# Score and value matmuls of a head pair entered as one piece in the list scheduler

## The chip, the cores and the metric

The kernel runs on one core of one Trainium2 chip. The metric is the time on the device for one execution, in microseconds (us). A program computes the kernel's own instruction order when the kernel is built, so the order is the same in every run.

## The reference

One layer of a hybrid decoder, for 512 tokens of width 1024, all in float32. The inputs are normalised and multiplied by one wide input matrix. The columns of the product go to two branches: an mLSTM with 4 heads of 128, and an attention with 8 heads of 64. The two branch outputs are gated, laid side by side, and multiplied by an output matrix into the residual. The change touches the attention alone. With two blocks of 256 tokens and up to three past blocks chosen, every earlier block is chosen, so it is causal attention with a linear bias:

```python
q = _rmsnorm(at_q.reshape(B, S, 8, 64), q_norm_w)
k = _rmsnorm(at_k.reshape(B, S, 8, 64), k_norm_w)
s = einsum('bhqd,bhsd->bhqs', q, k) * 64 ** -0.5 - slopes * distance   # causal
o_at = einsum('bhqs,bhsd->bhqd', softmax(s), v)
y_at = o_at.reshape(B, S, 512) * silu(at_z)
```

## The kernel before

**Arithmetic.** A float32 matrix product is made of three passes of a faster format: each operand is split in a high part and a low part (`whi`, `wlo` for weights; `xh`, `xl` for activations), and `mm3` issues high by high, high by low, low by high. ScalarE writes the high part, VectorE the low part.

**Attention.** `g_pair(p)` handles heads 2p and 2p+1, for p = 0 to 3. TensorE transposes q and k of both heads at once, so that head 2p lies on partitions 0 to 63 and head 2p+1 on partitions 64 to 127; ScalarE and VectorE split them into `qh`, `ql`, `kh`, `kl` (tiles named `br`). `g_attn` then makes:

- Scores. For each of four blocks of 128 queries (`g_tile(i)`), six matmuls: three passes for each of the two heads, alternating between the heads in program order. One contracts 64 rows, so it occupies half of TensorE's rows, and each head has a PSUM bank of its own. The width is 256, 256, 384 and 512 columns for i = 0 to 3. That is 16 such sets in the kernel, 96 matmuls, shown as `bank<-br,br 64*128`.
- Softmax (`g_soft`): VectorE adds the bias and takes the minimum, ScalarE exponentiates, GpSimd multiplies by the reciprocal sum; then TensorE transposes the result (`bank<-ident,b`) and ScalarE and VectorE copy it back.
- Values. For each of four blocks j of 128 keys, one matmul per head with 64 output columns, so it occupies half of TensorE's columns; the two heads write the two halves of the partitions of one bank, `acc`. The width is 512, 384, 256 and 128 columns. One float32 call gives two records in the trace: 64 records in the kernel, shown as `bank<-b,vbuf 128*64`.

**Order.** While `nc.on` is set, every engine call goes through `Schedule.add`, which runs nothing: it notes the engine, an estimated cost, and for each tile region which earlier operations must be done before it. `Schedule.issue` then places all operations by list scheduling: `place` gives each engine, whenever it is free in the plan, the ready operation that is most urgent, and the pass is repeated backward and forward 12 times; the placement of the shortest span is kept. All operations are then issued in the order of their planned starts. Each engine executes its own queue in that order and waits on semaphores where an input isn't there. The plan's cost of a matmul on half the rows is half that of a whole one, and on half the columns likewise (0.21 in place of 0.43), whatever stands beside it in the order.

**What lies around the change.** While the attention runs, TensorE's queue also holds the projections of the mLSTM's q and k and of the gate (`bank<-xh,whi` and the like, with activations moving and weights fixed; 128x512). `whi,xh` and the like are the projections with weights moving. After the attention come the mLSTM's own products and the output projection.

Every operation that the scheduler issues carries the line of the call in `Schedule.add`, L257, in the profile; so groups are told apart by their tiles.

Of the kernel before, what the change touches and what calls it, by code (L numbers as in the profile page):

```python
# [189 lines left out]
class Schedule:  # L190
# [10 lines left out]

    def __init__(self, nc):
        self.nc, self.on, self.ops, self.log = nc, False, [], {}
        for name in ("vector", "scalar", "gpsimd", "tensor", "sync"):
            setattr(self, name, Taker(self, name, getattr(nc, name)))

# [44 lines left out]
    def add(self, eng, name, fn, args, kw):  # L251
        aps = [a for a in (*args, *kw.values()) if isinstance(a, bass.AP)]
        out = kw.get("out", args[0] if args else None)
        outs = [r for r in (self.region(a) for a in (out, kw.get("accum_out")) if a is not None) if r]
        ins = [r for r in (self.region(a) for a in aps if a is not out and a is not kw.get("accum_out")) if r]
        dma = name.startswith("dma")
        op = {"eng": eng, "fn": lambda: fn(*args, **kw), "cost": self.cost(eng, name, out, ins, args, kw), "n": len(self.ops),  # L257
              "table": next((self.TABLES[a] for a in args if isinstance(a, AF) and a in self.TABLES), 0) if name == "activation" else 0,
              "pre": {}}
        self.ops.append(op)  # L260
        done = op
        if dma:
            size = 4.0
            for d in out.shape:
                size *= d
            done = {"eng": "dma", "fn": None, "cost": size / 524288.0 * (2900.0 if kw.get("accum_op") else 1480.0), "n": len(self.ops),
                    "table": 0, "pre": {op["n"]: 0.0}}
            self.ops.append(done)
        for reg, write in [(r, False) for r in ins] + [(r, True) for r in outs]:
            log = self.log.setdefault(reg[0], [])  # L270
            for r, w, o in log:
                if (w or write) and r[1] < reg[2] and reg[1] < r[2] and r[3] < reg[4] and reg[3] < r[4]:
                    if o["n"] in (op["n"], done["n"]):
                        continue
                    lat = self.LAT[o["eng"]] if o["eng"] != eng else 0.0 if eng == "tensor" else self.OWN if w else 0.0
                    op["pre"][o["n"]] = max(op["pre"].get(o["n"], 0.0), lat)
            if write:
                log[:] = [e for e in log if e[2] in (op, done) or not (reg[1] <= e[0][1] and e[0][2] <= reg[2] and reg[3] <= e[0][3] and e[0][4] <= reg[4])]
            log.append((reg, write, done))
# [57 lines left out]
    def issue(self, rounds=12):  # L337
        self.on = False
        self.tables()
        for o in self.ops:  # L340
            o["cost"] *= self.RESERVE.get(o["eng"], 1.0)
        n = len(self.ops)
        edges = [list(o["pre"].items()) for o in self.ops]
        back = [[] for _ in range(n)]
        for i, pre in enumerate(edges):
            for j, lat in pre:
                back[j].append((i, lat))
        zero = [0.0] * n
        span = lambda s: max(t + o["cost"] for t, o in zip(s, self.ops))
        best = start = self.place(edges, list(range(n)), zero)  # L350
        for _ in range(rounds):
            late = self.place(back, [-(t + o["cost"]) for t, o in zip(start, self.ops)], zero)
            start = self.place(edges, [-(t + o["cost"]) for t, o in zip(late, self.ops)], zero)
            if span(start) < span(best):
                best = start
        for i in sorted(range(n), key=lambda i: (best[i], i)):
            if self.ops[i]["fn"]:
                self.ops[i]["fn"]()


class Taker:
# [15 lines left out]
def hybrid_layer(ctx: ExitStack, tc: tile.TileContext, xT, x, w_in, w_out, smalls, out):  # L377
    nc = Schedule(tc.nc)
# [66 lines left out]
    for name, cols in _chunks():  # L445
        n = len(cols)
# [389 lines left out]
    def g_attn(p, qh, ql, kh, kl, t0):  # L836
        rank = 5 + p / 100
        yield when(lambda: b2.ok() and b5.ok(2) and (p < 2 or 2 * p - 3 in pts))
        eh, prs = b2.get(), [b5.get() for _ in range(2)]

        te = pool.tensor_scalar(eh, dist, 2.0 ** -(2 * p + 1), 0.0, op0=ALU.mult, op1=ALU.add)
        mn, sums, rec = ([tiny(NT) for _ in range(2)] for _ in range(3))
        done = {"p": [0, 0], "t": [0, 0]}
        at = [t0, t0]

        def finish(key, u, t):
            at[u] = max(at[u], t)
            done[key][u] += 1

        def g_tile(i):  # L850
            n = P * (i + 1)
            nn = max(n, 256)
            yield (max(*at, te), lambda: banks.ok(KEEP + 1), True)
            ps = [banks.get() for _ in range(2)]
            ts = slice(i * P, (i + 1) * P)
            now = plan.now
            for a, b in ((qh, kh), (qh, kl), (ql, kh)):
                for u in range(2):
                    r = slice(64 * u, 64 * u + 64)
                    mm(ps[u][:, :nn], a[r, ts], b[r, :nn], a is qh and b is kh, a is ql)  # L860
            plan.now = (now + plan.now) / 2
            for u in range(2):
                plan.add(g_soft(u, i, n, ps[u]), rank, plan.now + SLACK)

        def g_soft(u, i, n, ps):
            p_ = prs[u][:, offs[i]:offs[i] + n]
            t_ = dve.tensor_tensor_reduce(p_, ps[:, :n], eh[:, S - n:], scale=-0.5 if u else -1.0, scalar=BIG,
                                          op0=ALU.add, op1=ALU.min, accum_out=mn[u][:, i:i + 1])
            banks.put(t_, ps)
            yield t_  # L870
            yield act.activation(p_, p_, AF.Exp, scale=-1.0, bias=mn[u][:, i:i + 1], accum_out=sums[u][:, i:i + 1])
            have["exp"] += 1
            dve.reciprocal(rec[u][:, i:i + 1], sums[u][:, i:i + 1])
            yield dve.clock + SLACK
            finish("p", u, pool.tensor_scalar(p_, p_, rec[u][:, i:i + 1], 1.0, op0=ALU.mult, op1=ALU.mult))

        def g_pt(u, a, blocks, pt):
            yield pe_bank(at[u])
            ps = banks.get()
            n = P * len(blocks)  # L880
            for b, (i, j) in enumerate(blocks):
                transpose(ps[:, b * P:(b + 1) * P], prs[u][:, offs[i] + j * P:offs[i] + (j + 1) * P], ident)
            yield plan.now + SLACK
            t_ = (act.copy, dve.tensor_copy, act.copy)[a](pt[:, 512 * a:512 * a + n], ps[:, :n])
            banks.put(t_, ps)
            finish("t", u, t_)

        def g_turn(u):
            yield when(lambda: done["p"][u] == NT and b5.ok())
            pt = b5.get()  # L890
            for a, blocks in enumerate(([(0, 0), (1, 0), (2, 0), (3, 0)],
                                        [(1, 1), (2, 1), (3, 1), (3, 3)],
                                        [(2, 2), (3, 2)])):
                plan.add(g_pt(u, a, blocks, pt), rank)
            yield when(lambda: done["t"][u] == 3)
            b5.put(plan.now, prs[u])
            pts[2 * p + u] = (pt, [pt[:, 0:512], pt[:, 512:896], pt[:, 1024:1280], pt[:, 896:1024]], at[u])

        for i in range(NT):
            plan.add(g_tile(i), rank)  # L900
        for u in range(2):
            plan.add(g_turn(u), rank + u / 200)
        yield when(lambda: sum(done["p"]) == 2 * NT)
        b2.put(plan.now, eh)
        br.put(plan.now, qh, ql, kh, kl)
        h = 2 * p + 1
        yield when(lambda: h in pts and h - 1 in pts and have["v"] == NT)
        yield pe_bank(max(pts[h][2], pts[h - 1][2]))
        acc = banks.get()
        for j in range(NT):  # L910
            for g in (h - 1, h):
                r0 = 64 * (g % 2)
                mm(acc[r0:r0 + 64, j * P:], tv[:, j, g * 64:g * 64 + 64], pts[g][1][j], j == 0, j == NT - 1)
            plan.now -= 4 * (S - j * P) / 2.4
            if j < NT - 1:
                yield pe()
        b5.put(plan.now, pts[h - 1][0], pts[h][0])
        yield plan.now + SLACK
        banks.put(dve.tensor_copy(ot[:, h // 2], acc), acc)
        have["at"] += 1  # L920
# [554 lines left out]
    for n, name in enumerate(NAMES):  # L1475
        if name not in SUMS:
            continue
        tag, other, op = SUMS[name]
# [136 lines left out]
```

## Time and profile before

| | |
|---|---|
| median of 3 runs | 311.43 us |
| lowest | 311.09 us |
| the profiled execution: time | 310.9 us |
| the profiled execution: span from the first to the last instruction | 309.2 us |
| TensorE busy | 304.3 us (98%) |
| VectorE busy | 215.5 us (70%) |
| ScalarE busy | 169.7 us (55%) |
| GpSimd busy | 68.8 us (22%) |

The busy times are sums over the span. PE is TensorE's matmuls, PEld its weight loads, DVE VectorE, ACT ScalarE, POOL GpSimd. A matmul's duration in the trace runs from its start until its last column is through, and the next one starts before that; so the distance from one start to the next start, and not the duration, is what a matmul takes of TensorE's time. "x6" in a row of the timeline is six records of one group with nothing of another group between them.

### The profile page before, as it was taken

How to read it: one execution, taken by the hardware profiler on the slowest of the kernel's cores; microseconds unless marked ns; L12 is line 12 of the kernel's file. 1: busy time of each engine (PE TensorE's matmuls, PEld its weight loads, DVE VectorE, ACT ScalarE, POOL GpSimd, SP SyncE). 2: the span in 40 equal slices, each digit the busy share in tenths (PEclk: the TensorE clock that was granted, in tenths of full speed). 3: DMA queues.
4: the chain of work that ended last, by engine and by line, in shares of the span. 5: the costliest groups of instructions: out<-in, count | busy, mean ns of one | idle time of the engine just before them, and what ended most of it. 6: DMA issues, size and time to landing. Idle time of an engine off the chain costs nothing.

```text
span 309.2 us, 4351 instructions
## 1 busy us (share of the span) xinstructions
PE 304.3 (98%) x1566; PEld 238.2 (77%) x1566; DVE 215.5 (70%) x457; ACT 169.7 (55%) x309; POOL 68.8 (22%) x90
## 2 busy tenths in 40 slices
PE   8999999999999999999999999999999999999995
PEld 4999888888886676766668657898888988788884
DVE  4987997789784576795656876183117767989992
ACT  3675847972456644364544469569132334679600
POOL 4000202159500465002525021100101037222200
PEclk9999999999999999999999999999999999999999
DMA  6995887334061010130001321446327389965434
GB/s 203 394 414 193 180 259 146 61 136 136 0 207 67 1 65 11 62 138 2 0 3 68 118 86 32 105 134 209 86 50 191 119 281 227 260 128 89 62 120 159
DMA packets 13381, 40.19 MB, mean 130 GB/s; under 512 B 1584, under 2 KB 1840, under 8 KB 13360
## 3 DMA queue, kind: packets, MB, share of 16 engines
q1 hardware_dynamic: 10640, 32.05, 29.7%
q0 software_dynamic: 2720, 7.87, 14.6%
q8 instruction: 12, 0.20, 0.3%
q14 instruction: 9, 0.07, 0.1%
HBM read 37.81 MB, written 2.10 MB: 129 GB/s over the span
## 4 chain that ended last, share of the span: by engine, by line
PE 98%; DVE 0%; issue 0%
PE bank L257 97%; PE bank L370 1%; DVE b L257 0%; DVE rstdb L370 0%; DVE warm L370 0%
## 5 line engine op out<-in xcount | busy, mean ns | idle before, releaser
L257 PE MATMUL bank<-whi,xh 128*128 128x512 f32 (+2 forms) x220 | 71.1, 364 | 0.0
L257 PE MATMUL bank<-wlo,xh 128*128 128x512 f32 (+2 forms) x220 | 71.0, 358 | 0.0
L257 PE MATMUL bank<-whi,xl 128*128 128x512 f32 (+2 forms) x220 | 71.0, 360 | 0.0
L257 DVE TENSOR_TENSOR wlo<-raw,whi 128x1024 fp32r<-128x1024 f32 x35 | 42.5, 1220 | 21.8 <-ACT whi L257 21.7
L257 PEld LDWEIGHTS bank<-whi,xh 128*128 128x128 f32 x220 | 38.5, 191 | 7.6 <-issue 0.8
L257 ACT CAST whi<-raw 128x1024 fp32r<-128x1024 f32 x35 | 36.4, 1048 | 12.5 <-PE bank L257 12.5
L257 PEld LDWEIGHTS bank<-whi,xl 128*128 128x128 f32 x220 | 38.2, 188 | 6.6 <-issue 0.2
L257 PEld LDWEIGHTS bank<-wlo,xh 128*128 128x128 f32 x220 | 38.2, 188 | 6.2
L257 PE MATMUL bank<-xh,whi 128*128 128x512 f32 x96 | 41.1, 428 | 0.0
L257 PE MATMUL bank<-xh,wlo 128*128 128x512 f32 x96 | 39.4, 411 | 0.0
L257 PE MATMUL bank<-xl,whi 128*128 128x512 f32 x96 | 39.3, 409 | 0.0
L257 PE MATMUL bank<-whi,br 128*128 128x512 f32 x112 | 36.3, 397 | 0.0
L257 POOL TENSOR_SCALAR b<-b,tinies 128x128 f32<-128x128 f32 (+3 forms) x32 | 23.1, 732 | 44.1 <-DVE tinies L257 40.3
L257 DVE CUSTOM_DVE_ANT_0 b<-bank,b 128x128 f32<-128x128 f32 (+3 forms) x32 | 15.0, 485 | 17.8 <-PE bank L257 17.8
L257 ACT ACTIVATE b<-b,tinies 128x128 f32<-128x128 f32 (+3 forms) x32 | 17.8, 556 | 16.0 <-DVE tinies L257 16.0
L257 PEld LDWEIGHTS bank<-whi,br 128*128 128x128 f32 x112 | 21.0, 188 | 5.0
L257 PEld LDWEIGHTS bank<-xh,whi 128*128 128x128 f32 x96 | 18.1, 188 | 6.1 <-issue 2.4
L257 PEld LDWEIGHTS bank<-xh,wlo 128*128 128x128 f32 x96 | 18.0, 188 | 5.8 <-issue 2.3
L257 PE MATMUL bank<-wlo,br 128*128 128x512 f32 x56 | 22.3, 399 | 0.0
L257 PEld LDWEIGHTS bank<-xl,whi 128*128 128x128 f32 x96 | 18.1, 189 | 4.3 <-issue 1.8
L257 POOL TENSOR_TENSOR tinies<-tinies,mhalf 128x8 f32<-128x8 f32 (+1 forms) x12 | 18.3, 1546 | 7.0 <-DVE tinies L257 6.8
L257 PE MATMUL bank<-ident,b 128*128 128x128 f32 (+1 forms) x104 | 18.5, 267 | 0.0
(170 smaller groups left out, 467.2 us busy)
## 6 DMA issues: line engine op xcount, KB each, us to landing
raw<-in_w_in_dram SPq DMA_DIRECT2D x28, 512.0 KB, 3.3
raw<-in_w_out_dram SPq DMA_DIRECT2D x5, 512.0 KB, 4.1
vbuf<-in_x_dram SPq DMA_DIRECT2D x4, 512.0 KB, 8.3
out_dram<-b SPq DMA_DIRECT2D x7, 256.0 KB, 2.1
b<-in_w_in_dram SPq DMA_DIRECT2D x3, 520.0 KB, 7.2
raw<-in_w_out_dram POOLq DMA_DIRECT2D x3, 512.0 KB, 6.5
b<-in_x_dram POOLq DMA_DIRECT2D x6, 256.0 KB, 4.3
tq<-in_xT_dram SPq DMA_DIRECT2D x4, 256.0 KB, 5.3
```

Source lines behind the costliest of these rows:

```text
L257: op = {"eng": eng, "fn": lambda: fn(*args, **kw), "cost": self.cost(eng, name, out, ins, args, kw), "n": len(self.ops), "table": next((se ...
L370: return fn(*args, **kw)
```

## The change

`Schedule` gets a `bundle`. While it is `None`, nothing differs. When it is a list, the first operation added becomes the piece that is scheduled, and each later one adds its cost to it and its call to the piece's list of calls. What the later ones must wait for, and what waits for them, is noted on the piece. `issue` runs the calls of a piece one after another, so nothing else stands between them in TensorE's queue. Two places use it: the six score matmuls of one block of queries, and the two value matmuls of one block of keys. The set of instructions, their operands and the plan's total cost are as before.

```diff
         self.nc, self.on, self.ops, self.log = nc, False, [], {}
+        self.bundle = None
...
-        op = {"eng": eng, "fn": lambda: fn(*args, **kw), "cost": self.cost(eng, name, out, ins, args, kw), "n": len(self.ops),
+        call = lambda: fn(*args, **kw)
+        op = {"eng": eng, "fn": [call], "cost": self.cost(eng, name, out, ins, args, kw), "n": len(self.ops),
...
-        self.ops.append(op)
+        if self.bundle is not None:
+
+            if not self.bundle:
+                self.bundle.append(op)
+            elif op is not self.bundle[0]:
+                self.bundle[0]["cost"] += op["cost"]
+                self.bundle[0]["fn"].append(call)
+            op = self.bundle[0]
+        if op["n"] == len(self.ops):
+            self.ops.append(op)
...
-            if self.ops[i]["fn"]:
-                self.ops[i]["fn"]()
+            for fn in self.ops[i]["fn"] or ():
+                fn()
...
             now = plan.now
+            nc.bundle = []
             for a, b in ((qh, kh), (qh, kl), (ql, kh)):
                 for u in range(2):
                     r = slice(64 * u, 64 * u + 64)
                     mm(ps[u][:, :nn], a[r, ts], b[r, :nn], a is qh and b is kh, a is ql)
+            nc.bundle = None
...
         for j in range(NT):
+            nc.bundle = []
             for g in (h - 1, h):
                 r0 = 64 * (g % 2)
                 mm(acc[r0:r0 + 64, j * P:], tv[:, j, g * 64:g * 64 + 64], pts[g][1][j], j == 0, j == NT - 1)
+            nc.bundle = None
```

## Rows read from the trace of the kernel before

**Rows 1.** The page: span, busy times, granted clock in 40 slices, chain that ended last.
```profile
span 309.2 us, 4351 instructions
...
PE 304.3 (98%) x1566; PEld 238.2 (77%) x1566; DVE 215.5 (70%) x457; ACT 169.7 (55%) x309; POOL 68.8 (22%) x90
...
PEclk9999999999999999999999999999999999999999
...
PE bank L257 97%; PE bank L370 1%; DVE b L257 0%; DVE rstdb L370 0%; DVE warm L370 0%
```

**Rows 2.** Waits of PE (all there are): us in total, times, longest.
```profile
PE bank L370 <- DVE warm L370: 1.2, 1, 1.2
```

**Rows 3.** Timeline of PE, 150.2 to 151.6: start, us, operation.
```profile
150.16 0.40 PE L257 MATMUL bank<-xl,whi 128*128 128x512 f32 x1
150.40 0.39 PE L257 MATMUL bank<-xh,wlo 128*128 128x512 f32 x1
150.72 0.61 PE L257 MATMUL bank<-br,br 64*128 64x256 f32 x3
151.26 0.51 PE L257 MATMUL bank<-xh,whi 128*128 128x512 f32 x1
151.60 0.40 PE L257 MATMUL bank<-xl,whi 128*128 128x512 f32 x1
```

**Rows 4.** Timeline of PE, 103.2 to 109.9.
```profile
103.27 0.62 PE L257 MATMUL bank<-br,br 64*128 64x256 f32 x6
103.82 0.50 PE L257 MATMUL bank<-xh,whi 128*128 128x512 f32 x1
...
106.84 0.79 PE L257 MATMUL bank<-br,br 64*128 64x384 f32 x3
...
109.83 0.97 PE L257 MATMUL bank<-br,br 64*128 64x512 f32 x6
```

**Rows 5.** Timeline of PE, first and last stretch of scores, and one in between.
```profile
95.23 0.74 PE L257 MATMUL bank<-br,br 64*128 64x256 f32 x6
...
100.34 0.96 PE L257 MATMUL bank<-br,br 64*128 64x512 f32 x3
...
159.71 0.97 PE L257 MATMUL bank<-br,br 64*128 64x512 f32 x6
```

**Rows 6.** Busy time by stretch (window, its length, PE busy, records), tile br alone: scores.
```profile
95.00:102.00 7.00, 4.17 (x24) 1.00 0.00 1
102.00:111.00 9.00, 3.77 (x24) 1.00 0.00 0
...
150.00:161.00 11.00, 5.01 (x24) 1.00 0.01 2
```

**Rows 7.** The same, tile vbuf alone: values.
```profile
120.00:125.00 5.00, 3.45 (x16) 1.00 0.28 99
132.00:139.00 7.00, 3.44 (x16) 1.00 0.37 133
170.00:174.00 4.00, 2.60 (x16) 1.00 0.00 0
```

**Rows 8.** Timeline of PE, stretches of values of the second and the last pair.
```profile
132.79 1.07 PE L257 MATMUL bank<-b,vbuf 128*64 128x512 f32 x2
...
136.47 2.37 PE L257 MATMUL bank<-b,vbuf 128*64 128x512 f32 x14
...
183.31 1.72 PE L257 MATMUL bank<-b,vbuf 128*64 128x512 f32 x8
...
185.86 0.87 PE L257 MATMUL bank<-b,vbuf 128*64 128x256 f32 x8
```

**Rows 9.** Waits of all engines: us in total, times, longest.
```profile
DVE b L257 <- PE bank L257: 34.7, 27, 5.1
```

**Rows 10.** Timeline of DVE, the third pair's low parts.
```profile
136.86 1.41 DVE L257 SCALAR_TENSOR_TENSOR br<-bank,sm,br 128x512 fp32r<-128x512 f32 x2
```

**Rows 11.** Timeline of PE, the scores that follow them.
```profile
138.76 0.62 PE L257 MATMUL bank<-br,br 64*128 64x256 f32 x6
```

## The prediction

> **What bounds the kernel now.** I read the page first. TensorE is busy for 304.3 of 309.2 us, the chain that ended last lies 97% on TensorE's matmuls of line 257, and the granted clock is at its upper level, 2.4 GHz, in every slice [rows 1]. Next I asked for TensorE's waits. There is one, of 1.2 us, at the warm-up ahead of the first weights [rows 2]. From there until its last matmul TensorE never stands still for an input. So the time of the kernel is that wait, plus what the matmuls take one after another, plus a tail behind the last one (a VectorE step and the last store). Whatever shortens TensorE's own sequence shortens the kernel by as much, until something else fails to keep up.
>
> So the question is what the half-array matmuls take today. For that I read TensorE's timeline by starts. A whole matmul of 512 columns is followed by the next after 0.24 us (150.16, 150.40) [rows 3]. At 150.72 stand three score matmuls of 256 columns together, and the next matmul starts 0.54 us later [rows 3]. At 103.27 six of the same width stand together and take 0.55 us, until 103.82 [rows 4]. So six cost what three cost: in the six, each head's matmul has the other head's beside it, while the three run one after another with half of the rows unused. The last record of such a stretch reaches 0.07 us over the next start (0.62 of busy time against 0.55) [rows 4]. Taken off, three of 384 columns (0.79) take 0.72 us and six of 512 (0.97) take 0.90 [rows 4]; three of 512 take 0.96 - 0.07 = 0.89, the same as six [rows 5].
>
> There is a second cost, of a stretch as such. The step from a whole matmul into a stretch is 0.32 us (150.40 to 150.72), and the first whole matmul behind it takes 0.34 (151.26 to 151.60) [rows 3]. Against 0.24 each that is 0.08 + 0.10, and to the nearest tenth 0.2 us for each stretch of half-array matmuls, beside its own length.
>
> **The change, part by part.** *Scores.* The 96 matmuls stand in 22 stretches today; the first begins at 95.23, the last at 159.71 [rows 5]. The four pairs of heads are busy for 4.17, 3.77, 3.77 (the second row of 3.77, from 138 to 149, isn't shown) and 5.01 us [rows 6], together 16.72; less 22 x 0.07 it is 15.18 us from start to start. After the change there are 16 whole sets, for each pair two of 256 columns, one of 384 and one of 512. I have no whole set of 384. Three alone take 0.72, six of the other widths cost what three do, and the middle between 0.55 and 0.90 is 0.72 as well, so I take 0.72. If halves of 384 did not overlap at all, a set would be 1.43, and the sum would lose 4 x 0.71 = 2.8 us; at the widths on both sides they do overlap, so that end gets almost no weight. One pair: 0.55 + 0.55 + 0.72 + 0.90 = 2.72; four pairs 10.88. Gain: 15.18 - 10.88 = 4.3 us.
>
> *Score stretches.* From 22 to 16, at 0.20 each: 1.2 us. Where two sets happen to be neighbours it is a little more.
>
> *Values.* The first two pairs are busy for 3.45 and 3.44 us, the last two for 2.60 and 2.59 (only the first of these is shown) [rows 7]. The difference is what a missing partner costs. In the last pairs the records stand eight and eight, both heads together; in the second pair two of one head go alone at 132.79, and 14 in an uneven order follow at 136.47 [rows 8]. All together it is 12.08 us of busy time in 9 stretches; less 9 x 0.07, 11.45. A pair as the last two takes 2.60 - 2 x 0.07 = 2.46, four of them 9.84. Gain: 1.6 us. The stretches go from 9 to 8, another 0.2, if key blocks stay two by two. They needn't: a piece here is one key block. If all 16 stand alone, there are seven stretches more than today, 1.4 us lost in place of 0.2 won; if the four of each pair stand together, there are four, and 1.0 is won. I take 8, the pattern of the two undisturbed pairs, and keep both ends (1.6 us worse, 0.8 better).
>
> *The plan's own view.* A piece costs the sum of its parts, and these were already counted at half of a whole matmul; so the plan's total for TensorE is the same, and the real order now keeps to what the plan assumed. Everything else may be shuffled, since `place` meets fewer and longer pieces, the DMA issues on SP and GpSimd included. TensorE's whole matmuls take the same in any order, so a shuffle costs only where it makes TensorE wait. No row prices that; I take nothing, with the rivals below as the other end and no gain on the lower one, as no wait is left to be removed.
>
> *Later readiness.* A piece can't start before the last of its inputs: for scores the low parts of q and k and both banks, for values the transposed softmax of both heads. The queue is in order, so the projections behind a waiting piece would wait too, and with them VectorE and ScalarE, which read their banks. I take nothing, by the row of 138.76: VectorE ended the third pair's low parts at 136.86 + 1.41 = 138.27 us [rows 10], and the values from 136.47 kept TensorE busy until the six scores began [rows 8, 11]. Today the waiting is the other way round: VectorE is idle for 34.7 us in 27 places until TensorE has filled a bank [rows 9]. If that cover is gone, the transposes of the softmax are late next, and then the value matmuls.
>
> The sum: 4.3 + 1.2 + 1.6 + 0.2 = 7.3 us. The profiled execution's 310.9 becomes 303.6. The median of the runs, 311.43, lies 0.5 above that execution, so I forecast 304.1 us.
>
> **The rivals.** *Part of it lost (306.9).* TensorE gets through the attention 7 us sooner, while the softmax chains of VectorE, ScalarE and GpSimd keep their length and the projections that fill TensorE meanwhile are no more than before. Then the filling ends early, and TensorE waits at a transpose or a value piece. For it: the third pair's scores begin only 0.5 us after their low parts are written [rows 10, 11]. Against it: VectorE's 34.7 us of waiting for TensorE, and no wait of TensorE to begin with [rows 2, 9]. A wait of 0.7 us ahead of each pair's values would be 2.8 us: 306.9.
>
> *Key blocks apart (305.7).* The end worked out above, 1.6 us worse.
>
> *The halves overlap less than I think (306.9 to 310).* With no overlap at 384 columns alone it is 306.9; with none anywhere only the stretches are won, 1.4 us, and the change doesn't do what it says: 310.0. Sets of six that cost as much as three, at 256 and 512 columns, speak against both [rows 3 to 5]. The Trainium skill (TensorE: Matmul & The Clock Gate, Part 3, the measured speedups) gives 3.07 times for four row tiles of 512 columns, and not 4; at that efficiency two tiles would give 1.5 times, an estimate by which the sum would be some 3 us smaller. This case's trace disagrees for two tiles: 0.90 us for six of 512 columns and 0.89 for three, 2.0 times.
>
> *Slower.* One mechanism: pieces that wait at the head of TensorE's queue for the later of the two heads. There are 16 score and 16 value pieces. The gain is used up when each waits 7.3 / 32 = 0.23 us on average, and the kernel is 2% slower (317.7) at (7.3 + 6.2) / 32 = 0.42 us each. For it: the two value records at 132.79 went 3.7 us ahead of the other 14 [rows 8], so one head can be ready well before the other, and a piece that is put where the earlier head was would wait. Against it: the plan notes the inputs of both heads on the piece, and puts other work ahead of it.
>
> **How the numbers follow.** The forecast case, all or nearly all of the 7.3 kept, has 0.62. Part of it lost 0.18; key blocks apart 0.10; less overlap 0.03; slower by less than 2% 0.03, by more 0.04. The low end is 304.1, less 0.8 (key blocks four together), less 1.0 (five score sets that become neighbours, at 0.20): 302.3. The high end takes in the part lost at 306.9 and half a microsecond of shuffling, 307.4. About 2%, 6.2 us, is what a measurement of this kernel can tell from no change, so "faster" ends at 305.2, close above the forecast. Faster: 0.62. Within 2%: 0.18 + 0.10 + 0.03 + 0.03 = 0.34. Slower: 0.04.
>
> **What would show it.** The score records stand in sixes or multiples of six, in 16 stretches or fewer, and their busy time falls from 16.7 to about 12.0 us. The value records stand in fours or multiples of four, with about 10.4 us in place of 12.1. TensorE's busy time falls to about 297 us, it has no wait beyond the 1.2 us, and its clock stays. I am wrong if TensorE shows waits between the first scores and the last values, or if six of 384 columns take more than 0.72 us.

## The result, and the profile after

The changed kernel takes 302.74 us (median of 4 runs) against 311.31 us before (median of 4). One of the four runs before took 425.87 us; the other three have the median 311.20, and with them the ratio is 0.9728, with a 95% interval of 0.9709 to 0.9747. That is faster by 8.5 us. The forecast was 304.1 us, and 302.74 lies inside its range, 0.4 us above the low end. From one profiled execution to the other it is 310.9 to 302.68, 8.2 us; the account below is made on these two.

The page of the changed kernel (line 258 is what line 257 was before, and 381 what 370 was):

```profile
span 301.0 us, 4348 instructions
...
PE 296.0 (98%) x1566; PEld 234.9 (78%) x1566; DVE 214.9 (71%) x457; ACT 169.6 (56%) x309; POOL 67.1 (22%) x90
...
PEclk9999999999999999999999999999999999999998
...
PE bank L258 97%; DMA b<-in_w_in_dram 1%; DVE whi L258 0%; DVE b L258 0%; SPq L258 0%; SPq L381 0%
```

Against [rows 1], TensorE lost 8.3 us of busy time with the same 1566 matmuls, and is as full as before; the other engines' busy times are nearly the same. Its clock is at the same level. All waits of TensorE, and the wait of VectorE for it:

```profile
PE bank L381 <- DVE warm L381: 1.2, 1, 1.2
...
DVE b L258 <- PE bank L258: 28.6, 22, 5.3
```

The first is that of [rows 2] and still the only one. VectorE's waiting for TensorE [rows 9] fell from 34.7 to 28.6 us; it still follows.

Busy time of TensorE by stretch, the score matmuls alone, to be laid beside [rows 6]:

```profile
96.00:102.00 6.00, 3.00 (x24) 1.00 0.28 89
102.00:111.00 9.00, 2.99 (x24) 1.00 0.01 2
130.00:145.00 15.00, 2.99 (x24) 1.00 0.17 61
146.00:154.00 8.00, 2.73 (x24) 1.00 0.01 3
```

And the value matmuls, beside [rows 7]:

```profile
119.00:125.00 6.00, 2.38 (x16) 1.00 0.26 87
133.00:138.00 5.00, 2.38 (x16) 1.00 0.22 84
162.00:166.00 4.00, 2.60 (x16) 1.00 0.00 0
175.00:180.00 5.00, 2.59 (x16) 1.00 0.01 3
```

Scores went from 16.72 to 11.71 us, values from 12.08 to 9.95. Counted in the timeline, the scores stand in 15 stretches (runs of them with no other matmul between) and the values in 6. Three places of the timeline show the sizes: a set of six at 256 columns, a set of 384 that the forecast had not seen whole, and two sets that became neighbours.

```profile
96.79 0.62 PE L258 MATMUL bank<-br,br 64*128 64x256 f32 x6
97.34 0.50 PE L258 MATMUL bank<-xl,whi 128*128 128x512 f32 x1
...
98.75 0.79 PE L258 MATMUL bank<-br,br 64*128 64x384 f32 x6
99.47 0.50 PE L258 MATMUL bank<-xh,whi 128*128 128x512 f32 x1
...
151.10 1.49 PE L258 MATMUL bank<-br,br 64*128 64x384 f32 x12
152.52 0.50 PE L258 MATMUL bank<-xh,whi 128*128 128x512 f32 x1
```

Six of 384 columns take 0.72 us from start to start, what three took alone in [rows 4]. The two neighbours (six of 384, six of 512) take 1.42 us together, 0.20 less than 0.72 + 0.90. With 0.07 us taken off for each stretch, as in the forecast:

| | before | after | gain |
|---|---|---|---|
| scores, start to start | 15.18 | 11.71 - 15 x 0.07 = 10.66 | 4.5 |
| values, start to start | 11.45 | 9.95 - 6 x 0.07 = 9.53 | 1.9 |
| everything else of the profiled execution | 310.9 - 26.63 = 284.27 | 302.68 - 20.19 = 282.49 | 1.8 |

The last line is what remains, not a measurement of one thing. It has the entries and exits of the stretches, ten fewer than before (31 to 21), and a loss at the start: from the 13th matmul behind the warm-up on, the changed kernel runs 0.2 us later than the kernel before (7.59 us against 7.38), and the last line shown of its page puts a DMA of the first weights into the chain. So the ten bring 2.0 us, 0.20 each. The steps say the same: around a stretch they are some 0.33 and 0.34 us, where they are 0.24 between whole matmuls.

### The profile page after: what moved, and what is told of

Same layout as the page of the kernel before. It is cut to its first block, busy times and chain, and to the rows that moved or that the text cites. A ratio compares the mean times of both kernels' runs of the same rounds, so it can differ in the third digit from the quotient of the medians.

```text
span 301.0 us, 4348 instructions
## 1 busy us (share of the span) xinstructions
PE 296.0 (98%) x1566; PEld 234.9 (78%) x1566; DVE 214.9 (71%) x457; ACT 169.6 (56%) x309; POOL 67.1 (22%) x90
## 4 chain that ended last, share of the span: by engine, by line
PE 97%; DMA 1%; DVE 0%; SPq 0%; issue 0%
PE bank L258 97%; DMA b<-in_w_in_dram 1%; DVE whi L258 0%; DVE b L258 0%; SPq L258 0%; SPq L381 0%
## 5 line engine op out<-in xcount | busy, mean ns | idle before, releaser
L258 PE MATMUL bank<-xh,wlo 128*128 128x512 f32 x96 | 38.7, 403 | 0.0
L258 POOL TENSOR_SCALAR b<-b,tinies 128x128 f32<-128x128 f32 (+3 forms) x32 | 20.0, 632 | 35.1 <-DVE tinies L258 32.5
```

Of the source, the lines that this page charges most:

```text
L258: call = lambda: fn(*args, **kw)
```

## The experiments

The theory: TensorE is the bound, and the change wins by two things in its own sequence, namely the halves that run side by side, and the fewer entries and exits. Its rivals: all of it is entries and exits; or the order was shuffled luckily. Each run is compared with the kernel before on the same chip.

**Scores alone as pieces, and values alone.** In the first, the two `bundle` lines of the values are left out; in the second, those of the scores.

> Only the scores are kept as pieces. Theory: the score part of the gain stays (15 stretches), the values go back to 9 stretches with lone records: 1.9 us for their own length and 3 stretches at 0.2, so about 305.2 us. Rival (shuffle): no relation to the parts; anything between 302.7 and 311.3 us.

> Only the values are kept as pieces. Theory: the scores stand as before the change (22 stretches), the values in 7: 1.9 us of their own length and 2 stretches at 0.2 are won, about 309.0 us. The gains of this run and of the scores alone add up to that of both within 0.5 us. Rival (shuffle): they need not add up.

Measured: scores alone 305.30 us against 311.16 before, ratio 0.9813 (0.9798 to 0.9827); values alone 309.15 us, ratio 0.9934 (0.9919 to 0.9949). Both are as the theory sized them, to 0.2 us. The gains, 5.9 and 2.0, add to 7.9; both together gave 8.5. So they add up within 0.6 and not within the 0.5 that I had set. Two parts are seen, since the rest of the order matters to what becomes neighbours: with the values alone as pieces they stand in 7 stretches, with both in 6; and with the scores alone as pieces the values are busy for 12.29 us, 0.2 more than before the change. Luck of the order as the main cause is out: each part brings what its own matmuls say.

**One head after the other in a score piece.** The two loops change places, so the three matmuls of one head stand ahead of the three of the other.

```diff
-            for a, b in ((qh, kh), (qh, kl), (ql, kh)):
-                for u in range(2):
+            for u in range(2):
+                for a, b in ((qh, kh), (qh, kl), (ql, kh)):
```

> Inside each score piece the three matmuls of one head come first and then the three of the other, in place of taking turns; the instructions, the pieces and the order of everything else are those of the changed kernel. Theory (the gain is the overlap of the two halves): each six becomes serial. From the steps inside a lone stretch, three more matmuls cost 0.36 us at 256 columns, 0.52 at 384 and 0.69 at 512; 8 x 0.36 + 4 x 0.52 + 4 x 0.69 = 7.7 us more, 310.4 us. Rival (the gain is the fewer stretches, or a luckier order of the rest): 302.7 to 303 us, as the changed kernel.

Measured: 302.77 us, ratio 0.9731 (0.9715 to 0.9747). My expectation was wrong by 7.6 us, and the number is the rival's. Taken alone it would say that overlap has nothing to do with it. The timeline says otherwise:

```profile
96.81 0.63 PE L258 MATMUL bank<-br,br 64*128 64x256 f32 x6
97.37 0.50 PE L258 MATMUL bank<-xl,whi 128*128 128x512 f32 x1
...
96.81 0.39 PE L258 MATMUL bank<-br,br 64*128 64x256 f32 x2
```

The third row is the same stretch with the window closed at 96.83: two matmuls have begun by then, though in the queue the partner comes fourth, and the six take 0.56 us. So the halves overlap all the same. TensorE started the free half's matmul ahead of two that stood in front of it. That each engine executes its own queue in the order of issue, as the description of the kernel before has it, is not so here. What fell is my picture of how partners must stand, not yet the theory; it needed an experiment that really takes the overlap away.

**Both heads on one half.**

```diff
-                    r = slice(64 * u, 64 * u + 64)
+                    r = slice(0, 64)
```

> The changed kernel with both heads of a score piece on rows 0 to 63, so that the second head's scores are the first head's over again; the number, the widths and the order of all instructions stay. Theory (the overlap of the row halves pays): each six is serial; three more steps of 0.12, 0.17 and 0.23 us in the three widths, 8 x 0.36 + 4 x 0.52 + 4 x 0.69 = 7.7 us more than the changed kernel, 310.4 us. Rival (standing together without others between is all of it): 302.7 us.

Measured: 310.65 us, ratio 0.9981 (0.9964 to 0.9997). This kernel leaves out the second head's scores and does the first's twice. With all pieces kept and the order of TensorE's work the same, nearly the whole gain is gone. The timeline of it, from stretches at a granted clock of 1.00, to be laid beside the rows of 96.79 and 98.75 above:

```profile
98.44 0.97 PE L258 MATMUL bank<-br,br 64*128 64x256 f32 x6
99.34 0.49 PE L258 MATMUL bank<-xh,wlo 128*128 128x512 f32 x1
99.76 1.31 PE L258 MATMUL bank<-br,br 64*128 64x384 f32 x6
101.01 0.50 PE L258 MATMUL bank<-xh,whi 128*128 128x512 f32 x1
...
101.89 1.65 PE L258 MATMUL bank<-br,br 64*128 64x512 f32 x6
103.47 0.50 PE L258 MATMUL bank<-xh,whi 128*128 128x512 f32 x1
```

The sixes take 0.90, 1.25 and 1.58 us where they took 0.55, 0.72 and 0.90. So overlap of the row halves is worth 8 x 0.35 + 4 x 0.53 + 4 x 0.68 = 7.6 us, and 310.65 - 302.74 = 7.9 measures it. Six of 512 columns on one half take 1.76 times what they take on two, and not the 2.0 that the prediction read from three of them: the first and the last step of a stretch are longer (0.22 and 0.20 us at 256 columns, where one between is 0.12), and they are there once either way. (Part of that overlap the kernel before had already, which is why the change brought less for the scores.)

**Key blocks joined, and one head after the other there.** The four key blocks of a pair go into one piece: `nc.bundle = []` and `None` stand outside the loop over j, and the `yield` inside it is gone. In the second kernel the two loops change places as well.

> The changed kernel with the four key blocks of a pair's values in one piece. Theory: 4 stretches of values in place of 6 (0.4 us each with what refills and drains inside it), one stretch of scores more (0.4 the other way), one stretch of 36 rows less: 302.2 us. Rival (a longer piece holds up what is behind it): 303 us or more, with waits of TensorE.

> As the kernel with the joined key blocks, but in a piece all four matmuls of one head come first and then those of the other. Theory: the column halves no longer overlap; one head's eight records take 2 x (0.42 + 0.32 + 0.21 + 0.10) = 2.1 us, so 2.1 us more for each of four pairs, 8.4 us over the joined kernel, about 310.6 us. Rival: the same as the joined kernel.

Measured: joined 302.00 us, ratio 0.9702 (0.9686 to 0.9718); one head after the other 308.13 us, ratio 0.9901 (0.9886 to 0.9916). Both have 4 stretches of values and 16 of scores, and all other matmuls stand in the same order, so 6.1 us are overlap of the column halves and nothing else, less than the 8.4 expected without any overlap. The value matmuls of the first pair, joined, and then with one head after the other:

```profile
120.00:125.00 5.00, 2.38 (x16) 1.00 0.00 0
```

```profile
120.00:125.00 5.00, 3.93 (x16) 1.00 0.00 0
...
120.20 1.72 PE L258 MATMUL bank<-b,vbuf 128*64 128x512 f32 x4
...
121.43 0.97 PE L258 MATMUL bank<-b,vbuf 128*64 128x384 f32 x3
```

One pair takes 1.55 us longer. The second row holds the starts until 121.7: four records in a row. The third holds those from 121.43 to 121.8, where two more start together. So the later head's first record starts with the earlier head's fifth of eight, and from there on the two overlap. That record's own start is 121.764; until there it is 121.76 - 120.20 = 1.56 us, which is the whole difference.

**The look-ahead in the scores.** Everything joined (below), but in each piece one head's matmuls come first: six and six in a piece of two sets.

> As the kernel with everything joined, but in each score piece all matmuls of one head come first, then those of the other: six and six in the piece of the first two sets. From the values in turn, where the later head's first record started together with the earlier head's fifth of eight: TensorE starts a matmul of the free half when at most four records of the other half lie before it. So the seventh starts with the third, two steps of 0.12 us more in each of four pieces: 299.5 + 1.0 = 300.5 us. Rivals: it looks ahead without limit, 299.5 us; it looks ahead for three alone, 300.9 us; not at all, over 303 us.

Measured: 300.94 us, ratio 0.9674 (0.9632 to 0.9715), 1.4 us over its partner's 299.50. A piece of twelve of 256 columns, with the heads taking turns and then one after the other:

```profile
96.69 0.98 PE L258 MATMUL bank<-br,br 64*128 64x256 f32 x12
```

```profile
96.43 1.32 PE L258 MATMUL bank<-br,br 64*128 64x256 f32 x12
...
96.43 0.73 PE L258 MATMUL bank<-br,br 64*128 64x256 f32 x4
```

It is 0.34 us longer; four such pieces are the 1.4 us. The last row is the window closed at 96.79: four matmuls have begun, the third and fourth of them together (at 96.775 and 96.782 by the records' own starts). So the later head's first record starts with the earlier head's third, at the distance that I took from the values. What I had wrong is the price of the two steps until there: the first step of a stretch is longer, so they are 0.22 + 0.12 = 0.34 us (starts at 96.433, 96.656, 96.775) and not 2 x 0.12. That is the whole difference. The twelve starts fall into two runs of six with the same steps, the second (96.782, 97.010, 97.129, 97.241, 97.361, 97.481) 0.35 us behind the first. The time lies at the 300.9 of the rival with a look-ahead of three only because that number had the short first step too: by the starts, the later head would then have begun with the fourth record (96.892), 0.46 us late, 1.8 us in four pieces. So a look-ahead of four records fits the three runs with one head first. What exactly is counted, matmuls or their weight loads as well, is not shown.

**128 rows in the mLSTM's four small matmuls.** This tries the entry and exit by itself, with no halves in play. `sel` and `mrow2` get 128 rows, zeros beyond the 36.

```diff
-    mrow2 = sb("mrow2", [36, S], F32R)
+    mrow2 = sb("mrow2", [P, S], F32R)
...
-    sel = sb("sel", [36, MLH, P], F32R)
+    sel = sb("sel", [P, MLH, P], F32R)
```

> The changed kernel, with the four mLSTM matmuls that contract 36 rows widened to 128 rows by rows of zeros (no other matmul differs). Theory (a change of the number of rows or columns in use costs TensorE time by itself): the steps around the four, 0.32 to 0.43 us where whole ones take 0.23, fall to 0.23; nine steps, 1.2 us in all, 301.5 us. Rival (the steps are long for other reasons, such as a wait for the operand): 302.7 us.

Measured: 301.82 us, ratio 0.9699 (0.9685 to 0.9714), 0.9 us under the changed kernel. The same run of operations in the changed kernel, and with 128 rows:

```profile
170.37 0.39 PE L258 MATMUL bank<-xh,wlo 128*128 128x512 f32 x1
170.69 0.50 PE L258 MATMUL bank<-mrow,sel 36*128 36x512 f32 x1
...
173.44 0.39 PE L258 MATMUL bank<-whi,xl 128*128 128x512 f32 x1
```

```profile
170.93 0.40 PE L258 MATMUL bank<-xh,wlo 128*128 128x512 f32 x1
171.16 0.40 PE L258 MATMUL bank<-mrow,sel 128*128 128x512 f32 x1
...
172.90 0.40 PE L258 MATMUL bank<-whi,xl 128*128 128x512 f32 x1
```

3.07 us became 1.97, 1.1 of the expected 1.2, and the step into the first of them 0.23 in place of 0.32: the same arithmetic on more rows is faster here. The Trainium skill (TensorEngine Tiling (Array Packing), Tiling Modes) says that changing the tiling mode drains TensorE. These rows agree in that each change costs time, and price it; that it is a drain they don't show.

**Pieces of two.** `nc.bundle = []` stands inside the loop over passes, so a score piece is one pass of both heads.

> Scores kept together two by two (one pass, both heads) and no longer as six; values as in the changed kernel. Theory: what matters is that partners stand side by side; the plan's order has them in 15 stretches all the same, so 302.7 us within 0.5. Rival (a piece must be the whole set to pay): 304 us or more.

Measured: 303.22 us, ratio 0.9745 (0.9728 to 0.9761). Within the 0.5 us. The scores stand in 15 stretches here too; the values in 7 in place of 6 account for part of the rest. A piece need not hold all six: what pays is that partners stand side by side, in as few stretches.

**Longer pieces.** The first joins the first two score sets of a pair, joins the key blocks, and widens the four small matmuls. The second also joins the third and fourth sets.

```diff
-        for i in range(NT):
-            plan.add(g_tile(i), rank)
+        for tiles in ((0, 1), (2,), (3,)):        # second kernel: ((0, 1), (2, 3))
+            plan.add(g_tile(*tiles), rank)
```

> All of these together: the first two score sets of a pair in one piece, the four key blocks in one piece, 128 rows in the four mLSTM matmuls. Theory: 12 stretches of scores in place of 15 and 4 of values in place of 6, at 0.4 us each, and 1.2 us for the widened matmuls: 302.7 - 1.2 - 0.8 - 1.2 = 299.5 us. Rival (longer pieces make TensorE wait for inputs): 302 us or more, with waits of TensorE in the attention.

> As the kernel with everything joined, with the third and fourth score sets of a pair in one piece too. Theory (each stretch costs 0.4 us with what refills and drains inside it): 8 stretches of scores in place of 12, 1.6 us: 297.9 us. Rival (pieces that need four banks at once wait for VectorE to empty them): 300 us or more, with waits of TensorE during the attention.

Measured: 299.50 us, ratio 0.9624 (0.9610 to 0.9639), and 298.25 us, ratio 0.9567 (0.9543 to 0.9591). Four stretches fewer bring 1.25 us, 0.31 each, somewhat under the 0.4 (the kernels before on the two chips differ by 0.1). The second is 4.5 us faster than the change, and its page shows the bound unmoved:

```profile
span 296.5 us, 4343 instructions
...
PE 291.2 (98%) x1566; PEld 235.5 (79%) x1566; DVE 215.3 (73%) x457; ACT 168.5 (57%) x309; POOL 70.2 (24%) x90
```

Pieces that need four banks at once did not make TensorE wait in the attention. Its waits beside the warm-up:

```profile
PE bank L258 <- DVE whi L258: 0.4, 1, 0.4
```

That one is for the first weights at the start. It is 0.2 to 0.6 us in the profiled executions of the experiments and absent in that of the change, so differences of less than about half a microsecond between these kernels aren't read here.

## Why the prediction was right, point by point

- *The bound.* Right. TensorE had no new wait, and each kernel's time went with TensorE's own sequence, in both directions: 310.65 with the overlap taken away, 298.25 with fewer stretches.
- *Scores, 4.3 us.* It was 4.5. The open price of six at 384 columns came out as taken, 0.72; the end where they don't overlap is out. The 0.2 over is the two sets that became neighbours.
- *Score stretches, 22 to 16 at 0.20.* There are 15, and 0.20 us each outside their own length.
- *Values, 1.6 us, and 9 stretches to 8.* It was 1.9, and 9 to 6. This term was sized too small: I took the pattern of the two undisturbed pairs, two stretches each. In the first two pairs the four key blocks came to stand together, as at the low end that I had kept. Standing together saves twice: the entry and exit, and the longer first and last steps inside (2.38 against 2.60 of busy time). My 0.20 for a stretch had only the first. The rival of key blocks that stand apart is out. The pair of neighbours in the scores gives 0.20 for the second.
- *Sum.* 7.3 forecast, 8.2 in the profiled executions. The missing 0.9 lies in the two terms of the stretches and values: 3 stretches fewer than forecast, at 0.20 outside and about as much inside, less the 0.2 lost at the start, is about that. The other half microsecond between 304.1 and 302.74 is what the forecast added to get from the profiled execution to the median. It had no mechanism behind it: the median of the changed kernel lies 0.06 above its profiled execution.
- *Later readiness, and the rivals of lost time and of slower.* No wait of TensorE at a piece was seen, in the changed kernel or with longer pieces. VectorE still waits for TensorE, so the cover held. "The queue is in order" was too strong, as the run with one head after the other in a score piece showed; nothing in the sum hung on it.
- *Less overlap than I think.* Out, by the run with both heads on one half. Its price was a little high too: a set of six of 384 columns without overlap takes 1.25 us, where the prediction took 1.43. What the forecast said of how partners stand ("each head's matmul has the other head's beside it") is true of the kernel's own order, but the runs with one head after the other showed that it is not needed; what separated partners before was a whole matmul between them.

## What to carry to other kernels

Where TensorE is the bound and some matmuls use half of its rows or columns, count the stretches in the timeline and price them by starts: a half whose partner is behind a whole matmul costs as much as both, and each change of rows or columns in use costs some 0.2 us outside the stretch and up to as much inside (0.31 together, where four stretches fewer were measured by themselves). A scheduler that gives half-array matmuls half the price must also be told to keep partners together, and then it pays to make the runs longer, as long as the engines behind are waiting for TensorE and not the reverse (the reverse was not tried here). Zero rows that make a small matmul whole can be cheaper than leaving it small.

## What the runs showed of the hardware that was not expected

TensorE starts a matmul on a free half ahead of others that come before it in its queue: with three of one head ahead of three of the other, six still took 0.56 us from start to start (96.81 to 97.37) and the time of the kernel did not change (302.77 against 302.74). It looks only a little way ahead: with six records of one head in front, the other's first started with the third, and with eight, with the fifth, and a pair's values took 1.55 us longer. In both, four records of the first head had still to start or started at that moment.
